# A hybrid decoder layer with x loaded transposed, GpSimd's elementwise work of the first third on VectorE and ScalarE, and conv blocks that leave PSUM by one copy

## The chip, the cores and the metric

The kernel runs on one core of a Trainium2 chip. The metric is device time in microseconds. Three runs of the kernel before took 1224.8, 1224.88 and 1230.06 us; the median is 1224.88. The engines have these names in the profile: PE is TensorE (matmuls and transposes; PEld is its loading of weights), DVE is VectorE, ACT is ScalarE, POOL is GpSimd, SP is SyncE, which issues most DMAs.

## The reference

One decoder layer in float32: 1024 tokens, model width 1024.

```python
hn = rms_norm(h, norm_g[i]); proj = hn @ w_in[i]
rg_x, rg_gate, gq, gk, gv, gz, gb, ga, s5_u, s5_gate = split_columns(proj)
xr = causal_dwconv(rg_x, rg_conv_w[i], rg_conv_b[i])             # width 4
y_rg = rg_lru(xr, ...) * silu(rg_gate)                           # 512 channels
y_gdn = gdn_branch(gq, gk, gv, gz, gb, ga, gdn_conv_w[i], ...)   # 8 heads of 128
y_s5 = s5_ssm(s5_u, ...)                                         # 32 groups of 16 channels, 64 states
z5 = gelu(y_s5); y_s5 = z5 * sigmoid(z5 @ s5_w_glu + s5_b_glu) * silu(s5_gate)
h = h + concatenate([y_rg, y_gdn, y_s5]) @ w_out[i]
h = h + sigmoid(rms_norm(h, ple_norm_g[i]) @ ple_w_gate[i]) * (p[i] @ ple_w_proj[i])
return rms_norm(h, final_norm_g)
```

rg_lru has h_t = a_t h_(t-1) + sqrt(1 - a_t^2) (g_t x_t), with sigmoids r and g of block-diagonal products of the conv's output and a = exp(-8 r softplus(-lambda)). gdn_branch passes q, k, v through the same kind of conv and silu, normalizes q and k, and runs the gated delta rule; its decay between positions i and j is exp(gcum_i - gcum_j) for j up to i, 0 above.

## The kernel before, in words

**Precision and tiling.** Every large product is made of three: each float32 operand is split into a rounded part (hi) and its rest (lo), and hi·hi, lo·hi and hi·lo are summed in PSUM. The normalized x lies transposed in SBUF as hhi and hlo: 128 partitions (channels of one k-tile), 8 k-tiles, 1024 tokens. w_in comes in blocks of 128 output columns. A block is projected in two halves of 512 tokens, each 8 k-tiles × 3 products of 128x512, so 48 products a block (`project`, L426); its result has channels on partitions and tokens along the row. The pool `pp` has two PSUM banks for these halves. Each half leaves PSUM by a task called a drain, which runs on ScalarE.

**Weights.** `weight` (L394) loads one block (wraw), casts it to whi on ScalarE (L402) and subtracts on GpSimd for wlo (L404). The next block's task starts when a block's own is taken (`take`). There are two buffers of whi and wlo and one of wraw.

**x.** `norm_x` (L340) loads x in 8 tiles of 128 tokens by 1024 channels. For two tiles at a time ScalarE squares with a sum along the row (L368), VectorE computes the reciprocal root, VectorE (for 6 tiles, L387) or ScalarE and GpSimd (for 2, L383 and L385) multiply by it and by norm_g, and PE transposes the tile in eight 128x128 pieces (L197), from which `transpose_split` (L328) makes hhi on ScalarE (L336) and hlo on VectorE (L338). A half of the projections may begin when its four tiles are split. In the same stretch the projection of p (`ple_proj`, products named `ph`, `pl`) and the tables of S5 (`s5_base`, `s5_tables`) are made; `outer` (L830 to L834) computes the tables from products of 128x1024: one side on VectorE (names s_Q, s_tmp) and the other, `part_g`, on GpSimd (s_G, s_tmg).

**Blocks with a conv.** `project_conv` (L441) serves the RG-LRU's four blocks and the heads' q, k and v. Its drain copies the half into raw on ScalarE (L462, three zero columns ahead), then writes cy = w3·x + bias from PSUM on ScalarE (L465, L467); VectorE adds the three shifted products from raw (L452). cy has a single buffer, so a drain may only run once the previous user of cy is done (`busy`): in the RG-LRU that is its scan (L663).

**RG-LRU, decay, recurrence.** `rg_post` makes the gates and the scan; its steps max (L653), om = 1 - om (L655, GpSimd) and square root (L657) lie between the gate and the scan. `decay` (L583) makes, for each head, the 1024 columns of exp(gcum_i - gcum_j): a row broadcast by DMA, a subtraction and a triangular mask on GpSimd (L588, L591), Exp on ScalarE (L594), out to DRAM. `solve`, `levels` and `chain` then do the delta rule of a head: triangular inverses, and a recurrence with names V, Sm, R, kd, AQ, each step short 128x128 products on PE and short copies and products on VectorE and ScalarE.

**What sets the order.** The work is written as generators (`Task`), each with a lane (pe, v, a, g, d), and `tick` (L247) is called after each projection product: it prices what has been issued on each engine (`price`, `account`) and lets tasks take their next step when their inputs would be there and their engine free; PRIO gives priorities. `pin` fixes the resulting order of each engine. So the order is settled when the kernel is built, from prices, and each engine runs its own list in order. The projection blocks are issued in one fixed sequence: x0 s0 e0 g0 x1 … g3 (16 blocks of the RG-LRU and S5, with x the conv blocks and e, s, g gates and S5 input), then k of heads 0 to 2, then q, v, z of head 0, then the other heads'. A gdn head's recurrence is filled with the projections of later heads.

## Time and profile before

| | us |
|---|---|
| median of three runs | 1224.88 |
| profiled execution | 1232.72 |
| span of its instructions | 1231.0 |
| PE busy | 1126.6 (92%), 6197 matmuls |
| VectorE busy | 844.9 (69%) |
| ScalarE busy | 536.0 (44%) |
| GpSimd busy | 361.0 (29%) |
| mean granted clock of PE | 0.950 |

The profile is one execution, traced by the hardware. Busy is the time in which an engine had an instruction running; the matmuls overlap their weights' loading, and a busy PE may run at half its clock. The span is cut into five stretches below: up to the first wait for baT (start: x is normalized and split), to the last projection before head 0's recurrence, that recurrence, the other heads, and the out projection with the last part.

### The profile page before, as it was taken

To read this page: it belongs to the slowest core of one execution; us is meant where nothing else is said; L and a number is where in the kernel's file an instruction comes from. 1 tells how busy PE (TensorE), PEld (TensorE's weight loads), DVE (VectorE), ACT (ScalarE), POOL (GpSimd) and SP (SyncE) were. 2 spreads that over 40 slices of the span, in tenths; PEclk is the share of its full clock that TensorE was granted. 3 is DMA by queue.
4 is the path that set the end of the run, shared out by engine and by line. 5 is a ranking of instruction groups with operands and counts; after the bars stand their busy time and mean duration, and the time that the engine had idled before them with its cause. 6 is when DMAs were issued, how large, how long until landed. Compare 5 with 4: busy or idle time off the path is not lost. (4 is left out here: it accounts for less than half of the span.)

```text
span 1231.0 us, 17352 instructions
## 1 busy us (share of the span) xinstructions
PE 1126.6 (92%) x6197; PEld 915.5 (74%) x6197; DVE 844.9 (69%) x1986; ACT 536.0 (44%) x1070; POOL 361.0 (29%) x259
## 2 busy tenths in 40 slices
PE   6659979999969998899999999999988999999996
PEld 5437768778757777788888788888866878878885
DVE  7797697759688894697579857974655344263764
ACT  6514545452646543235443534354564233243432
POOL 4321523416133452011112111221165033044442
PEclk9778989999979998589999999999989999999999
DMA  7301326153465431112222221212255455364222
GB/s 286 120 26 53 97 57 189 54 155 103 135 194 172 148 109 46 31 63 58 76 63 69 69 73 48 86 31 74 102 197 176 166 190 184 122 207 144 89 88 84
DMA packets 81621, 136.49 MB, mean 111 GB/s; under 512 B 31104, under 2 KB 41536, under 8 KB 81536
## 3 DMA queue, kind: packets, MB, share of 16 engines
q1 hardware_dynamic: 80384, 131.20, 34.0%
q0 software_dynamic: 1152, 4.19, 0.9%
q8 instruction: 49, 0.80, 0.3%
q14 instruction: 36, 0.29, 0.1%
HBM read 98.50 MB, written 31.49 MB: 106 GB/s over the span
## 5 line engine op out<-in xcount | busy, mean ns | idle before, releaser
L194 PE MATMUL pp<-hhi,whi 128*128 128x512 f32 x768 | 318.0, 414 | 20.1 <-ACT cy L465 11.1
L194 PE MATMUL pp<-hhi,wlo 128*128 128x512 f32 x768 | 315.6, 411 | 2.1 <-POOL wlo L404 2.1
L194 PE MATMUL pp<-hlo,whi 128*128 128x512 f32 x768 | 316.5, 412 | 0.0
L404 POOL TENSOR_TENSOR wlo<-wraw,whi 128x1024 fp32r<-128x1024 f32 (+1 forms) x52 | 126.7, 2436 | 509.2 <-ACT whi L402 470.2
L194 PEld LDWEIGHTS pp<-hhi,whi 128*128 128x128 f32 x768 | 148.5, 193 | 51.4 <-ACT cy L465 12.4
L194 PEld LDWEIGHTS pp<-hhi,wlo 128*128 128x128 f32 x768 | 147.8, 193 | 31.5 <-issue 2.5
L194 PEld LDWEIGHTS pp<-hlo,whi 128*128 128x128 f32 x768 | 148.1, 193 | 30.0 <-issue 2.9
L452 DVE SCALAR_TENSOR_TENSOR cy<-raw,c_gdn_conv_w,cy 128x512 f32<-128x512 f32 x144 | 130.5, 907 | 13.8 <-ACT cy L465 13.3
L1454 DVE TENSOR_TENSOR mhl<-mr,mhl 128x512 fp32r<-128x512 f32 x64 | 59.2, 925 | 81.9 <-ACT mhl L1452 80.2
L1454 POOL TENSOR_TENSOR ws<-wsr,ws 128x512 fp32r<-128x512 f32 x48 | 67.4, 1407 | 141.0 <-ACT ws L1452 140.9
L194 PE MATMUL pg<-ws,mhl 128*128 128x512 f32 x384 | 101.1, 397 | 0.6 <-ACT mhl L1452 0.4
L194 PEld LDWEIGHTS pg<-ws,mhl 128*128 128x128 f32 x384 | 71.5, 188 | 19.6 <-DVE mhl L1454 1.4
L194 PE MATMUL pp<-ws,fth 128*128 128x512 f32 x256 | 80.6, 395 | 0.0
L1452 ACT CAST mhl<-mr 128x512 fp32r<-128x512 f32 x64 | 39.8, 621 | 86.3 <-DMA mr<-mix 49.9
L402 ACT CAST whi<-wraw 128x1024 fp32r<-128x1024 f32 (+1 forms) x52 | 52.7, 1014 | 52.0 <-DMA wraw<-in_w_blk 50.0
L462 ACT COPY raw<-pp 128x512 f32<-128x512 f32 x56 | 32.6, 583 | 67.8 <-PE pp L194 67.4
L1101 DVE TENSOR_TENSOR sT<-sW,sA 64x31 f32<-64x31 f32 (+15 forms) x124 | 58.9, 475 | 3.3 <-POOL raw L461 1.4
L194 PEld LDWEIGHTS pp<-ws,fth 128*128 128x128 f32 x256 | 48.1, 188 | 10.9
L1276 ACT ACTIVATE osq<-on 128x128 f32<-128x128 f32 x64 | 19.8, 309 | 76.3 <-DVE on L1273 60.3
L1452 ACT CAST ws<-wsr 128x512 fp32r<-128x512 f32 x48 | 29.7, 621 | 51.3 <-DMA wsr<-in_w_out 26.3
L1250 DVE TENSOR_SCALAR V<-pc,bp 128x128 f32<-128x128 f32 x64 | 22.2, 347 | 43.0 <-PE pc L194 42.5
L194 PE MATMUL pp<-ws,ftl 128*128 128x512 f32 x128 | 51.4, 401 | 0.0
(410 smaller groups left out, 2201.8 us busy)
## 6 DMA issues: line engine op xcount, KB each, us to landing
wraw<-in_w_blk SPq DMA_DIRECT2D x48, 512.0 KB, 3.9
mr<-mix SPq DMA_DIRECT2D x64, 256.0 KB, 3.0
dec<-dec SPq DMA_DIRECT2D x16, 512.0 KB, 4.7
wsr<-in_w_out SPq DMA_DIRECT2D x32, 256.0 KB, 2.9
xt<-in_x SPq DMA_DIRECT2D x8, 512.0 KB, 8.9
ppd<-po POOLq DMA_DIRECT2D x8, 512.0 KB, 3.6
gcb<-grow SPq DMA_DIRECT2D x8, 512.0 KB, 4.5
dec<-gcb SPq DMA_DIRECT2D x8, 512.0 KB, 2.9
```

Of the source, the lines that this page charges most:

```text
L194: self.nc.tensor.matmul(**kw)
L402: nc.scalar.copy(out=hi, in_=raw)
L404: nc.gpsimd.tensor_tensor(out=lo, in0=raw, in1=hi.bitcast(F32), op=ALU.subtract)
L452: nc.vector.scalar_tensor_tensor(out=y[:, sl], in0=raw[:, j + sl.start:j + sl.stop], scalar=wconv[:, j:j + 1], in1=y[:, sl], op0=ALU.mult, ...
L462: nc.scalar.copy(out=raw[:, 3 + 512 * half:3 + 512 * half + 512], in_=ps)
L1101: e.tensor_tensor(out=tv, in0=W[:, :n, j:j + 1].to_broadcast([64, n, m]), in1=A[:, j:j + 1, j + 1:].to_broadcast([64, n, m]), op=ALU.mult)
L1250: v.tensor_scalar(out=V, in0=p2, scalar1=bp[:, t:t + 1], scalar2=None, op0=ALU.mult)
L1276: nc.scalar.activation(out=sq, in_=on[:, t, :], func=AF.Square, accum_out=d["so"][:, t:t + 1])
L1452: nc.scalar.copy(out=hl[:, 0, :], in_=raw)
L1454: e.tensor_tensor(out=hl[:, 1, :], in0=raw, in1=hl[:, 0, :].bitcast(F32), op=ALU.subtract)
```

## The change

x arrives transposed from the host (a second input, xT, is x transposed; x itself is still read later), in 16 pieces of 128 channels by 512 tokens. ScalarE squares a piece; PE sums over channels with four products whose weights are 128x128 pieces of the squares and whose moving operand is one column of ones, so that the sums of 128 tokens lie on 128 partitions; VectorE adds over the k-tiles and takes the reciprocal root; four products with the identity spread it over all partitions and along the row (`rb`); and for each k-tile VectorE multiplies x by norm_g and rb, ScalarE casts to hhi, VectorE subtracts for hlo. `project` now waits for each half and k-tile (`hdone`), and the first block of weights is fetched between the halves of x.

GpSimd's subtractions for wlo, its side of the S5 tables and its half of the PLE split go to VectorE; om goes to ScalarE; max becomes the bias of the square root (`least`, 1e-30); the subtraction in `decay` becomes the bias of Exp, which is issued as eight pieces of 128 columns. In `project_conv` the drain is the copy into raw alone, and cy is made from raw, in SBUF, by the conv's task. Two steps of S5 may take a bank from either of two PSUM pools, silu of k waits for S5's tail, and prices and priorities of the planner are set anew (not shown; VectorE's fixed part is dearer by 0.06 to 0.07 us, GpSimd's by 0.06).

```diff
-    def norm_x(self, hpool, sp, startup):
+    def norm_x(self, hpool, sp, startup, key):
         nc = self.nc
...
         self.hlo = hpool.tile([P, KB, S], F32R, name="hlo")
...
         next(startup)
...
+        H = [slice(0, 512), slice(512, 1024)]
+        xt = [self.slot(tag, [P, S], "xt") for tag in ("dec", "dec", "AT", "AT", "raw", "raw", "qT", "qT")]
+        there = {}
+        for half in range(2):
+            if half:
                 next(startup)
...
+                next(startup)
+                self.fetch(key)
+                self.step(self.wtask[key])
+            for k in range(KB):
+                self.account()
+                nc.sync.dma_start(out=xt[k][:, H[half]], in_=self.i["xT"][k * P:(k + 1) * P, H[half]])
+                there[half, k] = self.account()
+            if not half:
+                g = self.load(sp, "norm_g", [P, KB])
+        sq = [self.slot(tag, [P, 2, 512], "xsq") for tag in ("cy", "kd")]
+        def squares(half, box, sums):
+            box.append(self.ps(self.psg, [P, 4, KB]))
+            for k in range(KB):
+                yield "a", lambda: there[half, k] <= self.now
+                z = sq[k % 2][:, k // 2 % 2]
+                nc.scalar.activation(out=z, in_=xt[k][:, H[half]], func=AF.Square)
+                sums.append(self.spawn(colsum(z, box[0], k), "pe", sums[-1:]))
+        def colsum(z, ss, k):
+            for t in range(4):
+                self.mm(out=ss[:, t, k:k + 1], lhsT=z[:, t * P:(t + 1) * P], rhs=self.ones[:, 0:1], start=True, stop=True)
+            yield
+        def scale(half, box, sums):
+            yield "v", lambda: len(sums) == KB and all(t.done for t in sums)
+            ss = sp.tile([P, 4], F32, name=f"xss{half}")
+            nc.vector.tensor_reduce(out=ss, in_=box[0], axis=mybir.AxisListType.X, op=ALU.add)
+            z = self.rstd_of(sp, ss, 1.0 / D, EPS, 4, f"xr{half}", 1)
             while True:
...
                     break
...
+            yield "pe", self.psg
+            rb = self.ps(self.psg, [P, 512], KB)
+            for t in range(4):
+                self.mm(out=rb[:, t * P:(t + 1) * P], lhsT=r[:, t:t + 1].to_broadcast([P, P]), rhs=self.ident, start=True, stop=True)
+            for k in range(KB):
+                self.spawn(split(half, k, rb), "v")
+        def split(half, k, rb):
+            x, hi, lo = (z[:, H[half]] for z in (xt[k], self.hhi[:, k], self.hlo[:, k]))
+            nc.vector.scalar_tensor_tensor(out=x, in0=x, scalar=g[:, k:k + 1], in1=rb, op0=ALU.mult, op1=ALU.mult)
+            yield "a"
+            nc.scalar.copy(out=hi, in_=x)
+            e, lane = nc.vector, "v"
+            yield lane
+            e.tensor_tensor(out=lo, in0=x, in1=hi.bitcast(F32), op=ALU.subtract)
+            self.hdone.add((half, k))
+            self.hleft[half] -= 1
+        for half in range(2):
+            box, sums = [], []
+            self.spawn(squares(half, box, sums), "a", room=lambda half=half: there[half, 0] <= self.now and self.room(self.psg))
+            self.spawn(scale(half, box, sums), "v", room=lambda sums=sums: len(sums) == KB)
...
         nc.scalar.copy(out=hi, in_=raw)
-        yield "g"
-        nc.gpsimd.tensor_tensor(out=lo, in0=raw, in1=hi.bitcast(F32), op=ALU.subtract)
+        yield "v"
+        nc.vector.tensor_tensor(out=lo, in0=raw, in1=hi.bitcast(F32), op=ALU.subtract)
         self.wts[key] = hi, lo
...
         for half in range(2):
-            self.wait(lambda: not self.hleft[half])
             sl = slice(512 * half, 512 * half + 512)
...
             for k in range(KB):
+                self.wait(lambda: (half, k) in self.hdone)
                 for w, h in ((whi, self.hhi), (whi, self.hlo), (wlo, self.hhi)):
...
-    def project_conv(self, blk, wconv, bias, act=None):
+    def project_conv(self, blk, wconv, bias, act=None, after=()):
         nc = self.nc
...
             sl = slice(512 * half, 512 * half + 512)
+            yield "a", lambda: all(t.done for t in busy)
+            nc.scalar.activation(out=y[:, sl], in_=raw[:, 3 + sl.start:3 + sl.stop], func=AF.Identity, scale=wconv[:, 3:4],
+                                 bias=0.0 if bias is None else bias)
+            yield "v"
             for j in (2, 1, 0):
...
             if act:
-                yield "a"
+                yield "a", lambda: all(t.done for t in after)
                 yield from act(y, raw, sl)
...
             nc.scalar.copy(out=raw[:, 3 + 512 * half:3 + 512 * half + 512], in_=ps)
-            yield
-            if bias is None:
-                nc.scalar.activation(out=y[:, sl], in_=ps, func=AF.Identity, scale=wconv[:, 3:4])
-            else:
-                nc.scalar.activation(out=y[:, sl], in_=ps, func=AF.Identity, scale=wconv[:, 3:4], bias=bias)
-        self.project(blk, evac, lambda: all(t.done for t in busy),
-                     lambda half: out.append(self.spawn(conv(half), "v", self.drains[-1:])))
+        self.project(blk, evac, lambda: not self.hleft[1],
+                     lambda half: out.append(self.spawn(conv(half), "d", self.drains[-1:])))
         self.cybusy = list(out)
...
         nc.sync.dma_start(out=self.grow.rearrange("h (t i) -> (h t) i", t=NT), in_=gr)
-        self.gc = gc
+        self.ngc = keep.tile([P, 64], F32, name="ngc")
+        nc.vector.tensor_scalar(out=self.ngc, in0=gc, scalar1=-1.0, scalar2=None, op0=ALU.mult)
...
         yield "g"
-        nc.gpsimd.tensor_tensor(out=gb, in0=gb, in1=self.gc[:, h * NT:(h + 1) * NT].unsqueeze(2).to_broadcast([P, NT, P]),
-                                op=ALU.subtract)
-        yield
-        nc.gpsimd.affine_select(out=gb, in_=gb, compare_op=ALU.is_ge, fill=-1e4, base=0,
+        nc.gpsimd.affine_select(out=gb, in_=gb, compare_op=ALU.is_ge, fill=-1e30, base=0,
                                 pattern=[[0, NT], [1, P]], channel_multiplier=-1)
         yield "a"
-        nc.scalar.activation(out=gb, in_=gb, func=AF.Exp)
+        for t in range(NT):
+            c = h * NT + t
+            nc.scalar.activation(out=gb[:, t, :], in_=gb[:, t, :], func=AF.Exp, bias=self.ngc[:, c:c + 1])
+            if t == 3:
+                yield
         yield "d"
...
         nc.vector.scalar_tensor_tensor(out=om, in0=r, scalar=1.0, in1=T, op0=ALU.add, op1=ALU.mult)
-        yield "v"
-        nc.vector.tensor_scalar(out=T, in0=T, scalar1=1e-30, scalar2=None, op0=ALU.max)
-        yield "g"
-        nc.gpsimd.tensor_scalar(out=om, in0=om, scalar1=-1.0, scalar2=1.0, op0=ALU.mult, op1=ALU.add)
         yield "a"
-        nc.scalar.activation(out=T, in_=T, func=AF.Sqrt)
+        nc.scalar.activation(out=T, in_=T, func=AF.Sqrt, bias=self.least)
+        yield
+        nc.scalar.activation(out=om, in_=om, func=AF.Identity, scale=-1.0, bias=1.0)
         yield "v"
...
             u = self.slot("AT", [P, 8, 8, 16], "s_tmg")
-            yield from outer(G, u, Ag[:, :, 1:9], cre, Bg[:, :, 1:9], cim, 8, g)
-            yield from outer(G0.unsqueeze(2), u[:, :, 0:1, :], Ag[:, :, 0:1], cre, Bg[:, :, 0:1], cim, 1, g)
+            yield from outer(G, u, Ag[:, :, 1:9], cre, Bg[:, :, 1:9], cim, 8, v)
+            yield from outer(G0.unsqueeze(2), u[:, :, 0:1, :], Ag[:, :, 0:1], cre, Bg[:, :, 0:1], cim, 1, v)
...
         next(q)
-        part = self.spawn(part_g(), "g", room=lambda: i == 0 or i - 1 in self.shifted)
+        part = self.spawn(part_g(), "v", room=lambda: i == 0 or i - 1 in self.shifted)
         yield
...
         for q in range(2):
-            yield "pe", self.psg
-            pt = self.ps(self.psg, [P, 4, P], 2)
+            yield "pe", lambda: self.room(self.psg) or self.room(self.psa)
+            pt = self.ps(self.psg if self.room(self.psg) else self.psa, [P, 4, P], 2)
             for k in range(4):
...
         for q in range(2):
-            yield "pe", lambda: shifted.done and self.room(self.psg)
-            pt = self.ps(self.psg, [P, 4, P])
+            yield "pe", lambda: shifted.done and (self.room(self.psg) or self.room(self.psa))
+            pt = self.ps(self.psg if self.room(self.psg) else self.psa, [P, 4, P])
             for k in range(4):
...
             yield
-        y, raw, cv = self.project_conv(16 + h, self.gcw[:, 8 + h, :], None, act)
+        y, raw, cv = self.project_conv(16 + h, self.gcw[:, 8 + h, :], None, act, self.posts[:3] if h < 2 else self.posts)
         d["k"] = self.spawn(self.k_post(h, cv), "d", after=cv[:1] + [self.decays[h]] + ([self.hd[h - 3]["levels"]] if h >= 3 else []))
...
             nc.scalar.copy(out=hi, in_=r)
-            e, lane = (nc.gpsimd, "g") if half else (nc.vector, "v")
+            e, lane = nc.vector, "v"
             yield lane
...
                 startup = self.ple_proj()
-                self.norm_x(hp, cp, startup)
-                self.fetch(order[0])
+                self.norm_x(hp, cp, startup, order[0])
                 g = self.spawn(self.gates(sb, cp), "d")
...
                 self.gdn_setup(cp)
+                self.posts = tiles
                 for h in range(HEADS):
...
     o["x"] = np.asarray(x)[0]
-    o["norm_g"] = np.asarray(norm_g)[0]
+    o["xT"] = o["x"].T
+    o["norm_g"] = np.asarray(norm_g)[0].reshape(KB, P).T
     w = np.asarray(w_in)[0]
```

**Head 0's recurrence on PE.** The rows are those of PE as the last projections ahead of the recurrence's first level end, before:

```order
L194 MATMUL pp<-hhi,wlo 128x512
L194 MATMUL pp<-hhi,whi 128x512
L194 MATMUL pp<-hlo,whi 128x512
L194 MATMUL pp<-hhi,wlo 128x512
L194 MATMUL pg<-Xs,AT 32x32 x16
L194 MATMUL pg<-M_3810,XT 32x32
L194 MATMUL pg<-XT,M_3810 32x32 x2
L194 MATMUL pg<-M_3810,XT 32x32
```

Here pp are projection products (pp<-hhi,wlo is the third of three), pg<-Xs,AT the first of the levels; 84 rows from there on hold no pp. After:

```order
L194 MATMUL pp<-hlo,whi 128x512
L194 MATMUL pp<-hhi,wlo 128x512
L197 MATMUL pg<-ident,kT 128x128
L194 MATMUL pp<-hhi,whi 128x512
L194 MATMUL pg<-Xs,AT 32x32 x16
L194 MATMUL pp<-hlo,whi 128x512
L194 MATMUL pc<-vn,XT 128x128
L194 MATMUL pp<-hhi,wlo 128x512
L194 MATMUL pg<-kT 128x128 x4
L194 MATMUL pp<-hhi,whi 128x512
L194 MATMUL pc<-V,kd 128x128
L194 MATMUL po<-V,AQ 128x128
```

Level products and the first of the chain (pc<-vn,XT, pc<-V,kd, po<-V,AQ) now stand between projections. The first pg<-Xs,AT is 43 rows further up, after 1147 projections of blocks, and pc<-vn,XT comes after 1169; before, both came after 1248. The last six rows of the chain of head 0 stand without projections in the new order too.

**The last piece of x on VectorE.** Before, from the last subtraction for hlo:

```order
L338 TENSOR_TENSOR hlo<-pg,hhi 128x4x128
L800 TENSOR_TENSOR s_small<-s_s_720 128x32
L801 SCALAR_TENSOR_TENSOR s_s_720<-s_s_720,s_c_719 128x32
L802 TENSOR_TENSOR s_c_719<-s_c_719 128x32
L803 TENSOR_TENSOR s_c_719<-s_c_719,s_small 128x32
L804 TENSOR_TENSOR s_R_721<-s_R_721 128x32
L779 TENSOR_SCALAR s_s_720<-s_s_720 64x32
L697 TENSOR_TENSOR s_tmp<-s_w,s_ki 128x8x16
L698 TENSOR_TENSOR s_tmp<-s_w,s_kr 128x8x16
L699 TENSOR_TENSOR s_w<-s_w,s_kr 128x128
L700 TENSOR_TENSOR s_w<-s_w,s_tmp 128x128
L701 TENSOR_TENSOR s_w<-s_w,s_ki 128x128
```

After, from the last but one:

```order
L402 TENSOR_TENSOR hlo<-xt,hhi 128x512
L847 TENSOR_TENSOR s_G<-s_w,s_Ag 128x1024
L849 TENSOR_TENSOR s_tmp<-s_w,s_Bq 128x1024
L849 TENSOR_TENSOR s_tmg<-s_w,s_Bg 128x1024
L851 TENSOR_TENSOR s_Q<-s_Q,s_tmp 128x1024
L851 TENSOR_TENSOR s_G<-s_G,s_tmg 128x1024
L847 TENSOR_TENSOR s_w<-s_w,s_Ag 128x128
L397 SCALAR_TENSOR_TENSOR xt<-xt,c_norm_g,pg 128x512
L849 TENSOR_TENSOR s_tmg<-s_w,s_Bg 128x8x16
L851 TENSOR_TENSOR s_w<-s_w,s_tmg 128x128
L402 TENSOR_TENSOR hlo<-xt,hhi 128x512
```

The last hlo stands behind the products of both sides of the first S5 table (L847 to L851), which are a later row before.

**The drain of the second conv block on ScalarE.** Before:

```order
L945 COPY s_V<-pg 128x512
L402 CAST whi<-wraw 128x1024 x2
L462 COPY raw<-pp 128x512
L467 ACTIVATE cy<-pp,c_rg_conv_b,c_rg_conv_w 128x512
L462 COPY raw<-pp 128x512
L467 ACTIVATE cy<-pp,c_rg_conv_b,c_rg_conv_w 128x512
L893 COPY s_uP<-pp 128x8x64
```

After:

```order
L674 ACTIVATE cy<-cy 128x1024
L482 COPY raw<-pp 128x512 x2
L418 CAST whi<-wraw 128x1024
L910 COPY s_uP<-pp 128x8x64
L468 ACTIVATE cy<-raw,c_rg_conv_b,c_rg_conv_w 128x512 x2
L910 COPY s_uP<-pp 128x8x64
L418 CAST whi<-wraw 128x1024
```

cy is written from raw and no longer from pp, and both copies out of pp stand ahead of both. whi is the cast of a block's weights, s_uP the drain of the S5 block that comes next; cy<-cy is om.

## Rows read from the trace of the kernel before

**Rows 1.** stretches: from:to length, busy us (instructions) PE PEld DVE ACT POOL, clock, DMA, GB/s

```profile
0.00:94.17 94.17, 56.70 (x241) 41.30 (x241) 76.44 (x213) 39.09 (x71) 33.16 (x32) 0.85 0.40 141
94.17:481.89 387.72, 354.44 (x1709) 286.27 (x1708) 308.58 (x583) 192.64 (x268) 138.48 (x87) 0.95 0.40 118
481.89:527.56 45.67, 38.73 (x322) 32.09 (x322) 24.68 (x100) 14.30 (x44) 2.78 (x4) 0.54 0.15 37
527.56:880.00 352.44, 347.39 (x2455) 292.15 (x2455) 259.80 (x729) 157.55 (x441) 63.84 (x53) 1.00 0.21 64
880.00:1231.00 351.00, 329.36 (x1477) 263.64 (x1475) 175.35 (x364) 132.44 (x247) 122.73 (x84) 0.98 0.46 151
```

**Rows 2.** waits of PE: engine, line <- releaser: us in total, times, longest

```profile
PE pg L197 <- DVE hlo L338: 20.6, 4, 10.4
PE pp L194 <- ACT cy L465: 11.1, 4, 6.8
...
PE pp L194 <- ACT cy L467: 8.9, 1, 8.9
...
PE pc L197 <- DVE baT L500: 5.0, 1, 5.0
PE pp L194 <- POOL wlo L404: 2.1, 1, 2.1
```

**Rows 3.** timeline of PE, projections: start, us, instruction, repeats [idle before <-releaser]

```profile
95.19 0.63 PE L194 MATMUL pp<-hlo,whi 128*128 128x512 f32 x1
95.62 0.63 PE L194 MATMUL pp<-hhi,wlo 128*128 128x512 f32 x1
...
475.74 0.39 PE L194 MATMUL pp<-hlo,whi 128*128 128x512 f32 x1
475.97 0.39 PE L194 MATMUL pp<-hhi,wlo 128*128 128x512 f32 x1
```

**Rows 4.** timeline of PE: transposes of x, and narrow products

```profile
50.43 0.60 PE L197 MATMUL pg<-ident,xt 128*128 128x128 f32 x4
50.78 0.48 PE L194 MATMUL pc<-pl,ph 128*128 128x512 f32 x1
...
109.99 0.33 PE L194 MATMUL pc<-gg,upper 128*128 128x64 f32 x2
110.15 0.39 PE L194 MATMUL pc<-gg,ones 128*128 128x64 f32 x2
```

**Rows 5.** timeline of DVE in the first stretch

```profile
26.41 2.40 DVE L725 TENSOR_TENSOR s_small<-s_small 128x32 f32<-128x32 f32 x1
28.85 0.19 DVE L726 SCALAR_TENSOR_TENSOR s_small<-s_small 128x32 f32<-128x32 f32 x1
...
67.61 0.74 DVE L452 SCALAR_TENSOR_TENSOR cy<-raw,c_rg_conv_w,cy 128x512 f32<-128x512 f32 x1
...
81.34 0.68 DVE L338 TENSOR_TENSOR hlo<-pg,hhi 128x512 fp32r<-128x512 f32 x1
...
91.75 1.21 DVE L832 TENSOR_TENSOR s_tmp<-s_w,s_Bq 128x1024 f32<-128x1024 f32 x1
```

**Rows 6.** timeline of ACT: the drain of a conv block that PE waits for

```profile
159.93 0.78 ACT L467 ACTIVATE cy<-pp,c_rg_conv_b,c_rg_conv_w 128x512 f32<-128x512 f32 x1 [4.32 <-DVE rr L663]
```

**Rows 7.** timeline of PE: the projection that follows that drain

```profile
160.77 0.79 PE L194 MATMUL pp<-hhi,whi 128*128 128x512 f32 x1 [8.94 <-ACT cy L467]
```

**Rows 8.** lines of POOL, 0 to 480 us: form, count | busy, mean ns | idle before, releaser

```profile
L404 POOL TENSOR_TENSOR wlo<-wraw,whi 128x1024 fp32r<-128x1024 f32 x27 | 67.5, 2502 | 177.3 <-ACT whi L402 166.3 <-PE pc L197 6.7 <-PE pg L194 4.2
```

**Rows 9.** timeline of POOL beside the first row of Rows 5

```profile
25.55 3.21 POOL L385 TENSOR_TENSOR xt<-xt,gb 128x1024 f32<-128x1024 f32 x1 [2.39 <-ACT xt L383]
```

**Rows 10.** lines of DVE, 0 to 480 us: conv products

```profile
L452 DVE SCALAR_TENSOR_TENSOR cy<-raw,c_gdn_conv_w,cy 128x512 f32<-128x512 f32 x48 | 47.8, 998 | 6.7 <-ACT cy L465 6.5
```

**Rows 11.** timeline of PE: the same product in two steps of head 0's recurrence

```profile
511.70 0.77 PE L194 MATMUL pc<-V,kd 128*128 128x128 f32 x2 [0.53 <-DVE V L1250]
...
515.47 0.77 PE L194 MATMUL pc<-V,kd 128*128 128x128 f32 x2 [0.54 <-DVE sT L1101]
```

More of the change, by code (lines that the diff above doesn't have):

```diff
@@ L55 @@
     AHEAD = (0, 0.3, 0.3, 0)
-    PRIO = dict(turn=2, drain=-1, save=-0.5, conv=1, gates=2, blocks=2, part_g=1, s5_out=1, shift=-1, k_post=1, q_post=1, v_post=-0.5, chain=1, chain_out=-1, finish=1, solve=1, levels=1, glu_prep=0.5, pre=1, glu_post=2, split_late=1, split_soon=-0.5, add=-0.5, ple_norm=2, s5_base=0.5, s5_tables=2, decay=2, decay_late=-1, wstream=-1, mstream=0.5)
+    PRIO = dict(squares=2, colsum=2, scale=2, split=2, drain=-1, save=-0.5, conv=1, gates=2, blocks=2, part_g=1, s5_out=1, shift=-1, k_post=1, q_post=1, v_post=-0.5, chain=1, chain_out=-1, finish=1, solve=1, levels=1, glu_prep=0.5, pre=1, glu_post=2, split_late=1, split_soon=-0.5, add=-0.5, ple_norm=2, s5_base=0.5, s5_tables=2, decay=2, decay_late=-1, wstream=-1, mstream=0.5)
     def __init__(self, tc, ins, out):
@@ L358, in turn @@
-        def turn(x, t):
-            tl = slice(t * P, (t + 1) * P)
-            yield from self.transpose_split(x, self.hhi[:, :, tl], self.hlo[:, :, tl], self.psg)
-            self.hleft[t // 4] -= 1
-        def rows(t0, n):
-            ss = sp.tile([P, n], F32, name=f"xss{t0}")
-            for t in range(n):
-                yield "a", lambda: there[t0 + t] <= self.now
-                junk = self.slot("cy", [P, D], "xsq")
-                nc.scalar.activation(out=junk, in_=xt[t0 + t], func=AF.Square, accum_out=ss[:, t:t + 1])
-            yield "v"
-            z = self.rstd_of(sp, ss, 1.0 / D, EPS, n, f"xr{t0}", 1)
+        H = [slice(0, 512), slice(512, 1024)]
```

38 lines of the change are left out of this document (7 added, 31 removed).

## The prediction

> **What bounds the kernel now.** I read the table of stretches first [rows 1]: busy time of each engine in five stretches, then TensorE's clock. TensorE (PE) is busy in nearly all of it, so the time is PE work plus PE idle, and the change can only gain from idle time or from clock. Idle time lies in three places: 0 to 94.17 us (56.70 busy, 37.5 idle), 94.17 to 481.89 (354.44 of 387.72, 33.3 idle), and after 880 (329.36 of 351.00), which the change hardly touches. From 527.56 to 880 PE is busy 347.39 of 352.44; nothing is to be had there. The fourth place is a matter of clock: 481.89 to 527.56 is 38.73 us of PE work at a granted clock of 0.54, near the lower of its two levels (1.2 of 2.4 GHz), so 38.73 × 0.54 = 20.9 us at full clock. That stretch holds no projection, only the recurrence of head 0: many short products, each waiting for VectorE.
>
> Then the list of what PE waited for [rows 2]. 20.6 us go to the split x (hlo, four waits). 11.1 + 8.9 = 20.0 us go to cy, written by ScalarE from PSUM: a drain that stands behind a recurrence of VectorE. 5.0 us go to baT. Only 2.1 us in the whole run go to wlo of GpSimd.
>
> The two prices of a projection are in [rows 3]: it repeats every 0.227 us at full clock (475.74 to 475.97), every 0.425 at the half clock (95.19 to 95.62).
>
> **Stage 1, x.** *Removed:* 64 transposes of 128x128. Four take 50.78 − 50.43 = 0.35 us [rows 4], so 16 × 0.35 = 5.6 us of PE; also the wait of a whole half for its last piece, since half 1 may begin when its first k-tile is split. *Added on PE:* 64 column sums, 128x1 with 128 columns of weights, and 8 broadcasts of 128x128. The trace has no 128x1 matmul; the nearest is a 128x64 with the same weights, two in 0.16 us there counted as one fp32 product (109.99 to 110.15) [rows 4]. Bounds: 0, if they fall in the 37.5 idle us, and 0.43 each at the half clock's price of a 512-column step [rows 3], 27.5 us. I take 64 × 0.16 = 10.2 us, the row that it is nearest to, and 8 × 0.09 for the broadcasts (the transposes' price). Net +5.3 us of PE work, nearly all of it ahead of 82 us, where PE idles.
>
> The Trainium skill, "TensorE: Matmul & The Clock Gate", section "Step-by-step: what each phase is for", says that the time to load weights follows their column count. By it a 128x1 product with 128 columns of weights is not the hundredth part of a wide one; if it did follow the moving columns, the 64 would cost under 1 us and the sum be some 5 us lower where they aren't hidden. The 0.16 us row has both loads in it and can't tell the two apart.
>
> *What the end of the stage does.* The last hlo ended at 82.0 us before (81.34 + 0.68) [rows 5]. In the new order of VectorE it stands behind five table products of 1.21 us [rows 5] (6 us) that came after it or were GpSimd's, while the squares leave ScalarE in 512-column pieces and two chains of rsqrt replace four. I take 82 to 86 us. By then 21 of the 24 products of half 1 are out, where none was: 21 × 0.227 = 4.8 us. baT is now needed after 66 projections and not 43, so 5.0 us go; the fourteen steps at half clock behind that wait (95.19 on) cost 14 × 0.2 = 2.8 us, which go too. 12.6 us saved, less about 6 for a later last hlo and the sums: **−6 us**, from −20 (no later hlo, all added PE work hidden, more of the 20.6 saved) to +15 (sums at 0.43, hlo at 90).
>
> **Stage 2, 94 to 482 us.** *Conv leaves by one copy.* The activation that wrote cy from PSUM had to wait till cy's last reader, the scan on VectorE, was done; in the rows the drain starts at 159.93, 4.32 us after ScalarE was free, ended by the scan [rows 6], and PE resumes at 160.77 after 8.94 us [rows 7]. With the copy into raw alone, PSUM waits for nothing that VectorE does. So 20.0 us of waits go, and with each the slow clock that followed (the stretch has 0.95). What is late next: VectorE, which is 308.58 of 387.72 us busy [rows 1], and whose longest chain is still scan, then conv.
>
> *wlo and the tables on VectorE.* Of the 27 wlo up to 480 us [rows 8] about 24 lie here: 24 × 1.21 = 29 us (price of a 128x1024 product of two SBUF operands, 91.75 [rows 5]). part_g four times: three of 1.21 and three an eighth as wide (0.3, a guess from their size), 4 × 4.5 = 18 us. The max goes, four times 1.21 at most, 4 us taken. Added to VectorE +43 us. Against it stands what GpSimd took from VectorE. At 26.41 a 128x32 product on VectorE lasted 2.40 us, the next one 0.19, while GpSimd's own product ran 25.55 to 28.76 [rows 5, 9]. And 48 conv products take a mean of 1.00 us [rows 10], where one of that shape took 0.74 (67.61) [rows 5]: 48 × 0.26 = 12 us. The 24 of the RG-LRU and the other forms with two SBUF operands (scans, tables, S5) I put at twice that, 25 us, an estimate by the same share. So VectorE stays about as full as it was (+43 − 37), and wlo itself takes 1.21 us where it took 2.50.
>
> The Trainium skill warns here: "Perfetto Trace Analysis", section "Optimizing Scalar/DVE Operations", says that VectorE and GpSimd share an SBUF read port, so that moving work between the two might not help, and that a full VectorE should rather hand work away. The trace agrees that they hold each other up (2.40 against 0.19 us); whether work comes back as time is the rival below.
>
> The other edits I cost at nothing, because the projections on PE cover them: decay's subtract goes from GpSimd into the bias of Exp, now eight pieces, and om goes to ScalarE, which is busy for only 192.64 of 387.72 us [rows 1]; were ScalarE late by it, the conv's copies would be, some 1 us for each of eight heads. The four subtracts of PLE on VectorE lie in the start's 37.5 idle us.
>
> Waits added: wlo now stands in VectorE's queue behind convs and scans. PE has one block's 48 × 0.227 = 10.9 us to spare, since the weights of the next block are fetched as this one starts. The sum: 20.0 gone, some 6 of clock gone, 8 come back as new waits for VectorE: **−18 us**, from −35 (all 33.3 idle us and clock) to +10 (the wlo late by 0.6 us in each of 47 blocks, 28, against the 18).
>
> **Stage 3, head 0's recurrence.** In the order before, the first of its products comes after all 1248 projections of its first part, and 84 rows of PE follow with none; now the levels come after 1147 and the chain's first product after 1169, woven between the rest. So 101 projections, 23 us, now lie beside a recurrence whose steps wait on VectorE: before, one step of the chain took 515.47 − 511.70 = 3.8 us, with a wait of half a us in each [rows 11]. At best the stretch shrinks to its 20.9 us of work, −24.8. The last few steps are still bare; I leave 8 to 9 us of that exposed: **−16 us**, from −25 to 0 (if PE, in order, waits at each step for VectorE).
>
> **The rest** is as before: 0, give or take 5.
>
> **Sum.** −6 − 18 − 16 = −40. The profiled execution took 1232.72 us (span 1231.0), so 1192.7. The median of three is 1224.88, 0.6% less: 1192.7 × 1224.88 / 1232.72 = **1185 us**.
>
> **Rivals.**
> *VectorE becomes the bound.* The +43 us count in full where the conv chains run, the lost contention doesn't come back there, and head 0 isn't ready earlier than PE reaches it: stage 3 gives 0, stage 2 −8, stage 1 −6. −14: 1218.7, on the median's scale 1211. For it: VectorE 308.58 busy of 387.72 already. Against: the 1.00 against 0.74 us of a conv product [rows 10, 5]. The page of the Trainium skill named above would have it so.
> *wlo late at every block (slower).* The place is PE's third product of a block, which needs wlo; VectorE is in order, and a scan, such as ended the 4.32 us of [rows 6], or a train of tables may stand ahead; behind wlo on that queue stand the convs that the next drains feed. The gain of 40 us is spent over 47 blocks at 40 / 47 = 0.85 us each, from there it is slower; at 1.2 us it is −40 + 56 = +16: 1248.7, 1241. For it: ScalarE's and VectorE's in-order queues made the 8.94 us wait [rows 7]. Against: a block's 10.9 us of lead, and only 2.1 us of such waits before [rows 2].
> *No change.* The column sums come at the half clock and the last hlo late, +15; stage 2 −8, stage 3 −7: 0, 1225.
>
> **Numbers.** Forecast 0.62 (own range 1165 to 1205), VectorE 0.20, slower 0.11, no change 0.07. All three terms at their low ends would give 1145, at their high ends 1250; three ends at once are unlikely. The range reaches to 1226 to take in the VectorE case and no change and down to 1160; left out are the slower case and small tails. About 0.5% (6.1 us) is what three runs from 1224.8 to 1230.06 can tell. Faster 0.80 (0.02 of the VectorE case falls under the bound), same 0.09, slower 0.11.
>
> **What would show it.** Right: no wait of PE for cy; the last hlo at 82 to 86 us; conv products near 0.8 us; a granted clock near 1 after 482 us, with projections up to within 10 us of the end of head 0's chain. Wrong: waits of PE for wlo or for x in hundreds of ns per block, column sums of 0.4 us, a bare stretch of recurrence at half clock as long as before, or VectorE over 90% busy before 480 us.

## The result, and the profile after

The changed kernel took 1245.76 us in the median of four runs (1243.39 to 1249.87), the kernel before 1226.78 in its four; the ratio is 1.0156 [1.0117, 1.0194]. Forecast was 1185, so the sign was wrong.

Stretches, cut at the same places of the work in both kernels: the first product of block 1, of block 19 (q of head 0), of block 26 (after head 0's recurrence) and of block 47 (the last). The third stretch so holds some 96 us, of the kernel before, that the prediction counted to its second stage. Columns as in [rows 1]; before:

```profile
0.00:97.32 97.32, 59.85 (x248) 43.78 (x249) 78.15 (x218) 39.09 (x71) 33.16 (x32) 0.84 0.39 137
97.32:385.93 288.61, 260.26 (x1279) 209.36 (x1277) 226.01 (x392) 143.86 (x180) 97.28 (x60) 0.95 0.41 119
385.93:527.56 141.63, 129.76 (x749) 106.52 (x747) 105.54 (x285) 63.08 (x132) 43.98 (x31) 0.83 0.30 94
527.56:881.63 354.07, 349.02 (x2465) 293.50 (x2464) 260.74 (x731) 157.55 (x441) 63.84 (x53) 1.00 0.21 64
881.63:1231.00 349.37, 327.73 (x1468) 262.30 (x1466) 174.41 (x362) 132.44 (x247) 122.73 (x84) 0.98 0.46 152
```

After:

```profile
0.00:105.92 105.92, 79.54 (x320) 62.83 (x321) 64.74 (x211) 39.94 (x71) 9.18 (x20) 0.85 0.36 121
105.92:400.73 294.81, 259.88 (x1310) 209.94 (x1309) 216.57 (x479) 157.86 (x227) 12.82 (x19) 0.95 0.43 124
400.73:525.82 125.09, 109.96 (x725) 89.76 (x723) 83.23 (x243) 63.68 (x141) 9.46 (x17) 0.95 0.30 88
525.82:879.88 354.06, 348.12 (x2453) 294.10 (x2453) 253.29 (x751) 157.50 (x438) 12.66 (x30) 1.00 0.21 66
879.88:1244.60 364.72, 337.13 (x1478) 270.22 (x1476) 180.68 (x371) 133.39 (x250) 114.62 (x80) 0.96 0.42 144
```

By these, +8.6 us at the start (forecast −6), +6.2 in the middle (−18), −16.5 round head 0's recurrence (−16, its clock back at 0.95), 0.0 in the heads, and +15.3 at the end (0), where of the edited code only four subtractions for wlo and half a conv block stand.

The waits of PE after, as in [rows 2]:

```profile
PE pg L194 <- DVE s_X L989: 13.6, 1, 13.6
PE pg L194 <- ACT xsq L369: 10.9, 1, 10.9
PE pg L194 <- DVE AT L1093: 9.2, 1, 9.2
PE pp L194 <- ACT hhi L399: 8.3, 5, 2.2
...
PE pp L194 <- DVE hlo L402: 3.9, 4, 1.6
```

No wait for cy is left, and none for wlo. s_X, which is the last S5 tile's state, now has the longest wait.

PE meets that wait in a hole between projections. In both kernels the code has, behind the k blocks (block 18 is their last), `self.need(*tiles, *outs)`: block 19 is laid out only when all steps of S5 have been laid out. Before, from the last product of block 18 to the first of block 19:

```profile
382.65 0.39 PE L194 MATMUL pp<-hhi,wlo 128*128 128x512 f32 x1
385.01 1.16 PE L194 MATMUL pg<-kT 128*128 128x128 f32 x8 [1.97 <-DVE AT L1076]
385.93 0.48 PE L194 MATMUL pp<-hhi,whi 128*128 128x512 f32 x1
```

After, with the row of the stretch between:

```profile
357.84 0.39 PE L194 MATMUL pp<-hhi,wlo 128*128 128x512 f32 x1
...
391.38 0.77 PE L194 MATMUL pg<-s_X,s_G 128*128 128x128 f32 x2 [13.62 <-DVE s_X L989]
...
400.73 0.48 PE L194 MATMUL pp<-hhi,whi 128*128 128x512 f32 x1
```

```profile
357.84:400.73 42.89, 13.34 (x82) 12.36 (x81) 22.32 (x72) 14.71 (x34) 5.92 (x5) 0.68 0.46 117
```

At the end of block 18 PE was 25 us ahead of the kernel before; at block 19 it was 15 us behind. The hole has 13.34 us of PE's work in 42.89 us.

VectorE's conv and scan, against [rows 10] and, for the scan, this row of the kernel before:

```profile
L663 DVE TENSOR_TENSOR_SCAN rr<-cy,rT 128x1024 f32<-128x1024 f32 x4 | 13.3, 3324 | 0.2
```

After:

```profile
L472 DVE SCALAR_TENSOR_TENSOR cy<-raw,c_gdn_conv_w,cy 128x512 f32<-128x512 f32 x39 | 29.2, 753 | 9.1 <-ACT cy L468 5.8 <-issue 3.1
...
L680 DVE TENSOR_TENSOR_SCAN rr<-cy,rT 128x1024 f32<-128x1024 f32 x4 | 9.1, 2285 | 0.9 <-ACT cy L674 0.8
```

A conv product fell from 998 to 753 ns and a scan from 3324 to 2285: VectorE's own pace came back, as forecast.

The start, on PE: column sums at its early pace, and later (four sums are eight instructions):

```profile
13.60 1.70 PE L194 MATMUL pg<-ones,xsq 128*128 128x1 f32 x8
15.16 0.78 PE L194 MATMUL pp<-ph,pl 128*128 128x512 f32 x1
...
50.99 0.95 PE L194 MATMUL pg<-ones,xsq 128*128 128x1 f32 x8
51.80 0.48 PE L194 MATMUL pg<-ph,pl 128*128 128x512 f32 x1
```

That is 0.39 and 0.20 us a sum. And the last pieces of x on VectorE, which [rows 5] had done at 82.0:

```profile
95.73 0.69 DVE L402 TENSOR_TENSOR hlo<-xt,hhi 128x512 fp32r<-128x512 f32 x1
96.34 1.22 DVE L847 TENSOR_TENSOR s_G<-s_w,s_Ag 128x1024 f32<-128x1024 f32 x1
...
100.88 1.22 DVE L851 TENSOR_TENSOR s_G<-s_G,s_tmg 128x1024 f32<-128x1024 f32 x1
...
103.64 0.69 DVE L402 TENSOR_TENSOR hlo<-xt,hhi 128x512 fp32r<-128x512 f32 x1 [0.16 <-ACT hhi L399]
```

### The profile page after: what moved, and what is told of

It reads as the page before. It is cut to its first block, busy times and chain, and to the rows that moved or that the text cites. A ratio compares the mean times of both kernels' runs of the same rounds, so it can differ in the third digit from the quotient of the medians.

```text
span 1244.6 us, 17541 instructions
## 1 busy us (share of the span) xinstructions
PE 1134.6 (91%) x6277; PEld 926.8 (74%) x6277; DVE 798.5 (64%) x2051; ACT 552.4 (44%) x1127; POOL 158.7 (13%) x166
## 5 line engine op out<-in xcount | busy, mean ns | idle before, releaser
L472 DVE SCALAR_TENSOR_TENSOR cy<-raw,c_gdn_conv_w,cy 128x512 f32<-128x512 f32 x144 | 107.3, 746 | 11.3 <-ACT cy L468 7.3
L1471 DVE TENSOR_TENSOR mhl<-mr,mhl 128x512 fp32r<-128x512 f32 x64 | 53.2, 833 | 93.1 <-ACT mhl L1469 93.1
L420 DVE TENSOR_TENSOR wlo<-wraw,whi 128x1024 fp32r<-128x1024 f32 (+1 forms) x52 | 63.1, 1213 | 46.6 <-ACT whi L418 44.1
L194 PE MATMUL pp<-ws,mhl 128*128 128x512 f32 x192 | 52.5, 408 | 3.2 <-ACT mhl L1469 2.1
L1293 ACT ACTIVATE osq<-on 128x128 f32<-128x128 f32 x64 | 19.6, 307 | 64.9 <-DVE on L1290 50.0
```

The source lines that it names most:

```text
L194: self.nc.tensor.matmul(**kw)
L420: nc.vector.tensor_tensor(out=lo, in0=raw, in1=hi.bitcast(F32), op=ALU.subtract)
L472: nc.vector.scalar_tensor_tensor(out=y[:, sl], in0=raw[:, j + sl.start:j + sl.stop], scalar=wconv[:, j:j + 1], in1=y[:, sl], op0=ALU.mult, ...
L1293: nc.scalar.activation(out=sq, in_=on[:, t, :], func=AF.Square, accum_out=d["so"][:, t:t + 1])
L1471: e.tensor_tensor(out=hl[:, 1, :], in0=raw, in1=hl[:, 0, :].bitcast(F32), op=ALU.subtract)
```

## The experiments

Times are medians; ratios are to the kernel before, measured on the same chip. Differences in us are between medians, some of them from different chips; the median of the kernel before lay between 1226.8 and 1228.7 there, so 2 us between two runs say nothing. "x as before" is rows, transposes and the old split; "the old prices" are those of the planner before. X·G is the product of an S5 tile's state s_X with its table s_G.

**Undoing one part of the changed kernel.**

`u_x`: the diff of `norm_x`, `hleft` and `project` taken back, as

```diff
...
+            self.wait(lambda: not self.hleft[half])
...
-                self.wait(lambda: (half, k) in self.hdone)
...
```

> The changed kernel with x loaded in rows again, transposed and split as before; all else as changed. Theory 1 (the S5 chain is the bound of the first 400 us, and the new start, with its 64 column sums and with x's pieces in turn with the S5 tables on VectorE, sets it back): the first X·G product of S5 comes about 10 us earlier (185 to 175), the last gelu of S5 likewise, and the kernel takes 8 to 12 us less than the changed one, 1234 to 1238. Rival (VectorE's work in the first stretch is what counts, not x): within 4 us of the changed kernel.

1221.36, 0.9932 [0.9908, 0.9956]: 24 us. Block 1 started at 78.7 us, not 105.9; but S5's first X·G product only 6 us sooner (179.2), its last gelu 26 us (384.6). The start is confirmed, its size twice what I expected.

`u_price`:

```diff
-            return 0.16 + n / (460 if op == "InstTensorTensor" else 860)
+            return 0.1 + n / (445 if op == "InstTensorTensor" else 860)
...
-        return (0.19 if op == "InstTensorScalarPtr" and n > 64 else 0.14) + n / 960
+        return (0.13 if op == "InstTensorScalarPtr" and n > 64 else 0.07) + n / 960
```

> The changed kernel with the planner's old prices. Theory 2 (the 15 us lost after 880 us, where no instruction was changed, come from another order of the last head's products and of the streams behind them, which the planner's new prices set): the stretch from the last block's first product to the end goes back from 365 towards 349 us, the rest stays, and the time is 1230 to 1236. Rival (that order follows from where the earlier work left off, whatever the prices): the tail stays within 5 us of 365.

1211.53, 0.9856 [0.9828, 0.9884]: 34 us, with the same instructions (17541 in both profiles). Its stretches, cut at the same places:

```profile
0.00:105.74 105.74, 87.03 (x313) 69.65 (x314) 60.43 (x205) 38.05 (x69) 9.18 (x20) 0.94 0.35 121
105.74:389.05 283.31, 259.06 (x1317) 209.25 (x1316) 222.03 (x488) 156.58 (x221) 9.56 (x18) 0.96 0.44 125
389.05:508.20 119.15, 108.94 (x725) 89.34 (x724) 89.41 (x250) 64.41 (x149) 11.89 (x20) 0.94 0.33 101
508.20:857.50 349.30, 346.58 (x2461) 291.90 (x2460) 255.52 (x744) 161.92 (x441) 12.46 (x28) 1.00 0.22 66
857.50:1209.50 352.00, 330.39 (x1468) 264.69 (x1466) 177.61 (x366) 131.82 (x247) 117.02 (x80) 0.97 0.45 149
```

The end (block 47 on) took 352.0 us and not 364.7, but that is 13 of the 34; of the rest 11.5 lie in the middle, 5.9 round head 0 and 4.8 in the heads, and none at the start. From the first product of block 47 to the first of the out projection it took 60.9 us and not 69.64. Lines of VectorE in that stretch (form, count | busy, mean ns | idle before, releaser), of the changed kernel and then of this one:

```profile
L1308 DVE TENSOR_TENSOR on<-on,ory 128x512 f32<-128x512 f32 x3 | 5.5, 1841 | 0.0
...
L1267 DVE TENSOR_SCALAR V<-pc,bp 128x128 f32<-128x128 f32 x10 | 3.5, 349 | 10.7 <-PE pc L194 10.7
```

```profile
L1267 DVE TENSOR_SCALAR V<-pc,bp 128x128 f32<-128x128 f32 x8 | 2.8, 346 | 9.6 <-PE pc L194 9.6
...
L1308 DVE TENSOR_TENSOR on<-on,ory 128x512 f32<-128x512 f32 x2 | 2.5, 1235 | 0.0
```

With the dear price ten steps of the recurrence (V) and three finishing products (on) were left when the last block began, with the old one eight and two: the recurrences stand later between the projections, and their last steps are bare for longer.

`u_partg`:

```diff
-            yield from outer(G, u, Ag[:, :, 1:9], cre, Bg[:, :, 1:9], cim, 8, v)
+            yield from outer(G, u, Ag[:, :, 1:9], cre, Bg[:, :, 1:9], cim, 8, nc.gpsimd)
...
-        part = self.spawn(part_g(), "v",
+        part = self.spawn(part_g(), "g",
```

> The changed kernel with GpSimd's side of the four S5 tables back on GpSimd; all else as changed. Theory 1 (VectorE serves both x's pieces and the S5 tables, and both are late by it): the last hlo comes 5 to 10 us sooner than 104 us, S5's last gelu before 405 us instead of 410, and the time falls by 5 to 10 us, to 1236 to 1241. Rival (GpSimd's port costs VectorE what the tables cost): within 3 us.

1241.84, 1.011 [1.0083, 1.0138]: 4 us, and the last hlo later (112.1): the theory's mechanism isn't seen; inconclusive.

`u_decay`, the diff of `decay` taken back, of which this is the Exp:

```diff
...
-        for t in range(NT):
-            nc.scalar.activation(out=gb[:, t, :], in_=gb[:, t, :], func=AF.Exp, bias=self.ngc[:, c:c + 1])
...
+        nc.scalar.activation(out=gb, in_=gb, func=AF.Exp)
```

> The changed kernel with decay as before: the subtraction on GpSimd and one Exp of 1024 columns, not eight pieces with a bias. Theory 3 (S5's last tile is late by 19 us since ScalarE, in order, waits 5.6 us for a decay's row and mask at 331 us with S5's copies behind it, and SP's queue waits for Exp likewise): the last tile's period, from X·G of the third to X·G of the fourth, falls from 71.5 us towards 53, and the time by 8 to 15 us, to 1231 to 1238. Rival (the waits move with the planner's order and aren't of decay's making): that period stays above 65 us and the time within 5 us.

1234.9, 1.0045 [1.0023, 1.0067]: 11 us, but the period was 64.9 us: between the two, and `uxp_udecay` below speaks for the rival.

**Both large ones, and the rest on that base.** `ux_uprice` is `u_x` with the old prices.

> The changed kernel with both x as before and the planner's old prices. Theory 1+2 (the start cost 25 us and the prices 34, at different places): the two add up, 1246 - 25 - 34 = 1187, between 1182 and 1195. Rival (both free the same S5 chain, so the second finds little left): 1200 to 1211.

1181.28, 0.9638 [0.9604, 0.9673]: they add up, and 65 us separate it from the changed kernel. Its stretches to block 47:

```profile
0.00:83.90 83.90, 56.59 (x248) 41.20 (x249) 66.13 (x223) 39.77 (x71) 14.86 (x21) 0.90 0.46 159
83.90:360.58 276.68, 256.67 (x1303) 208.35 (x1301) 220.48 (x483) 154.72 (x220) 10.97 (x19) 0.97 0.46 130
360.58:473.90 113.32, 107.38 (x723) 88.08 (x723) 89.03 (x254) 64.54 (x148) 11.72 (x20) 0.98 0.34 101
473.90:824.87 350.97, 347.81 (x2462) 292.94 (x2462) 253.65 (x740) 161.66 (x441) 11.73 (x28) 1.00 0.22 66
```

Against before: −13.4, −11.9, −28.3, −3.1 us. In the second of them the hole ahead of block 19 is still there: the last product of block 18 began at 333.08 and the first of block 19 at 360.58, 27.5 us apart.

`uxp_uconv`, the diff of `project_conv` taken back (with it goes the wait of k's silu for S5's tail):

```diff
...
+                nc.scalar.activation(out=y[:, sl], in_=ps, func=AF.Identity, scale=wconv[:, 3:4], bias=bias)
-        self.project(blk, evac, lambda: not self.hleft[1],
+        self.project(blk, evac, lambda: all(t.done for t in busy),
...
```

> x as before, the old prices, and the conv blocks leave PSUM as before, by the copy and by the activation that waits for cy; the moves off GpSimd stay. My step said that the one copy frees 20 us of PE's waits for cy and some clock. Theory 5 (it does, and PE's time in the first 390 us hangs on it): 15 to 25 us slower than 1181, waits of PE for cy near 20 us. Rival 5b (S5's chain sets block 19, so PE that is free earlier waits there): within 6 us of 1181.

1201.34, 0.9783 [0.9761, 0.9806]: the one copy is worth 20 us, and waits for cy are back, 14.2 us in place of the 20 that I expected:

```profile
PE pp L194 <- ACT cy L465: 14.2, 2, 9.3
```

`uxp_uwlo_upartg`, with `u_partg`'s edit and

```diff
...
-        nc.vector.tensor_tensor(out=lo, in0=raw, in1=hi.bitcast(F32), op=ALU.subtract)
+        nc.gpsimd.tensor_tensor(out=lo, in0=raw, in1=hi.bitcast(F32), op=ALU.subtract)
```

> x as before, the old prices, and wlo and GpSimd's side of the S5 tables back on GpSimd; the conv by one copy, decay, the RG-LRU's edits stay as changed. Theory 4 (work taken from GpSimd comes back to VectorE as shorter products, so the move is worth its VectorE time): 10 to 20 us slower than the kernel with both undone and the moves kept, conv products at 0.85 us or more in place of 0.75. Rival (the port gives back just what the moves cost): within 4 us of it.

1211.07, 0.9858 [0.982, 0.9897]: the two moves off GpSimd are worth 30 us together. With them VectorE runs 76 instructions more (2063 against 1987) and is busy for less, 805.3 us against 824.8. Conv products took 797 and 843 ns here, scans 2698; of heads and RG-LRU, in this kernel:

```profile
L456 DVE SCALAR_TENSOR_TENSOR cy<-raw,c_gdn_conv_w,cy 128x512 f32<-128x512 f32 x45 | 35.9, 797 | 17.1 <-ACT cy L452 16.7
...
L456 DVE SCALAR_TENSOR_TENSOR cy<-raw,c_rg_conv_w,cy 128x512 f32<-128x512 f32 x24 | 19.8, 843 | 2.8 <-ACT cy L452 2.7
```

The heads' conv products, at 797, stay under the 850 that the theory asked for: most of their fall from 998 is there with wlo and the tables on GpSimd. The larger differences are in 128x1024 products of the RG-LRU and of S5, such as this one, here and then in `ux_uprice`:

```profile
L660 DVE SCALAR_TENSOR_TENSOR rT<-rr,rT 128x1024 f32<-128x1024 f32 x4 | 9.2, 2306 | 2.2 <-ACT rT L656 2.2
```

```profile
L660 DVE SCALAR_TENSOR_TENSOR rT<-rr,rT 128x1024 f32<-128x1024 f32 x4 | 4.9, 1219 | 0.0
```

How much of the 30 us comes by these, how much by wlo being ready sooner, and which of the two moves gave it, isn't shown; with the new prices the tables alone back on GpSimd were 4 us faster, not slower (`u_partg`).

`uxp_udecay`, with `u_decay`'s edit:

> x as before, the old prices, and decay as before (subtraction on GpSimd, one Exp). In the changed kernel that edit cost 11 us. Theory 3 (eight Exp pieces and their table loads on ScalarE are a loss wherever they stand): 1168 to 1176 against 1181. Rival 3b (that loss hung on the dearer prices' order): 1179 to 1190.

1184.94, 0.9655 [0.9624, 0.9685]: no loss here. What decay costs hung on the plan it stood in.

**What of x costs.** `split0_uprice`, with the old prices and

```diff
-    PRIO = dict(squares=2, colsum=2, scale=2, split=2, ...
+    PRIO = dict(squares=2, colsum=2, scale=0, split=0, ...
```

> The changed kernel with the old prices, x transposed as changed, and the planner's priority of scale and split at 0 and not 2, so that VectorE takes x's pieces ahead of the S5 tables. Theory 1a (the new start is late since x's pieces and the S5 tables, at equal priority, take turns on VectorE): the last hlo comes at 75 to 85 us and not at 102, block 1 at 85 to 92 and not 106, the time 1192 to 1203 against 1211. Rival 1b (the start is late from PE's column sums at half clock and the late first projections): block 1 stays after 100, the time 1207 to 1215. Rival 1c (the tables are then late, and S5's chain with them): the last hlo comes early but X·G of the first tile later than 187, and the time is 1207 or more.

1206.99, 0.9831 [0.9792, 0.987]. The last hlo came at 75.2, not 102.2, and bought 4.5 us, within the intervals: theory 1a fell. Block 0 still began at 72.7 and X·G at 184.3.

`cs32r`, with the old prices and

```diff
-        sq = [self.slot(tag, [P, 2, 512], "xsq") for tag in ("cy", "kd")]
+        sq = [self.slot(tag, [P, 2, 512], "xsq", F32R) for tag in ("cy", "kd")]
+        one = sp.tile([P, 2], F32R, name="onr")
...
-                self.mm(out=ss[:, t, k:k + 1], lhsT=z[:, t * P:(t + 1) * P], rhs=self.ones[:, 0:1], start=True, stop=True)
+                self.mm(out=ss[:, t, k, :], lhsT=z[:, t * P:(t + 1) * P], rhs=one, start=True, stop=True)
```

> The changed kernel with the old prices, and the squares and the column of ones rounded to fp32r (two columns of ones, one pass in place of two); the sums are then those of rounded squares. Theory 1b (the column sums' own PE time, 0.39 us each at half clock, holds up the first projections): they take half, block 0 starts some 10 us sooner than 80.5, and the time is 1200 to 1206 against 1211. Rival (S5's tables on VectorE set the start's length, PE has slack): block 0 sooner or not, block 19 within 3 us of 389 and the time within 4 us of 1211.

1195.75, 0.9733 [0.9706, 0.976]: 16 us. Four sums took 0.71 us at the early pace, not 1.56:

```profile
13.50 0.85 PE L194 MATMUL pg<-onr,xsq 128*128 128x2 f32 x4
14.21 0.77 PE L194 MATMUL pp<-ph,pl 128*128 128x512 f32 x1
```

Block 0 began at 53.5, not 80.5. By the spacing of the rows on PE ahead of block 0, the sums took 8.3 us in all and not 25.1, and the 112 products of 512 columns that both kernels have there took 32.5 us and not 40.8. So PE's own time for the sums was two thirds of the 27 us, and its pace nearly all of the rest: with the float32 sums among them, products stood 0.43 us apart till 68 us in `u_price`,

```profile
66.94 0.63 PE L194 MATMUL pp<-pl,ph 128*128 128x512 f32 x1
67.37 0.63 PE L194 MATMUL pp<-ph,pl 128*128 128x512 f32 x1
...
68.11 0.40 PE L194 MATMUL pp<-pl,ph 128*128 128x512 f32 x1
68.34 0.40 PE L194 MATMUL pp<-ph,pl 128*128 128x512 f32 x1
```

and in `cs32r` they first came to 0.23 at 24.5 us, with 22 of the 112 at the slow spacing and not 57. Why the pace rose later there isn't shown.

`price1`, with the old prices and, in `price`,

```diff
+            if n == 1:
+                return 0.2
```

> The changed kernel with the old prices, but the planner prices a product with one moving column at 0.2 us and not at 0.01. Theory 1d (the planner laid out the first 50 us as if 64 column sums took no time, so that PLE's products and copies stand in the way of block 0): block 0 starts 8 us or more before 80.5, and the time is 1200 to 1206. Rival (PE's time is spent whatever the plan): block 0 at 77 or later, and the time 1207 to 1214.

1205.56, 0.9818 [0.9787, 0.9848]: block 0 came at 68.5, and the time is 6 us less than with the old prices alone, though the intervals touch. A plan that knows the sums' price is perhaps part of it.

`x_best`: `cs32r` with `scale=0, split=0` and a price of 0.1 for the two-column product.

> x transposed, old prices, rounded squares and ones (the sums of rounded squares), their products priced at 0.1 us, and scale and split at priority 0. If the start's loss is the column sums and the plan that took them for free, this equals x as before, 1178 to 1186; if transposed x has another cost (two roots' chains in series with 16 casts and subtractions), it stays at 1190 to 1197.

1175.69, 0.9573 [0.9548, 0.9597], the fastest of all, with the squares in the norm rounded: with cheap sums transposed x costs nothing against x as before (0.9638), and perhaps gains a little.

**What of the prices costs.** `u_pdve`: VectorE's old price alone.

> The changed kernel with VectorE's old price alone, GpSimd's new. Theory 2a (VectorE's dearer fixed part makes the planner put products later behind VectorE than need be, and spread VectorE's steps): nearly all of the price's 34 us come back, 1209 to 1218. Rival 2b (GpSimd's price, or any small change, shuffles the order): 1225 or more.

1212.73, 0.9878 [0.9856, 0.9901]: it is VectorE's.

`p_late` is `ux_uprice` with

```diff
+        if self.count > 2256:
+            return (0.19 if op == "InstTensorScalarPtr" and n > 64 else 0.14) + n / 960
```

and `p_early` has `<=` there; 2256 projection products are those of the blocks 0 to 46.

> x as before, and the dearer VectorE price only from the last projection block on (the last head's recurrence, the out projection, PLE). Theory 2 (the tail's loss is those prices at work there): 12 to 18 us above 1181, with 47 us and more from block 47 to the first out product in place of 60, all of the loss behind block 47. Rival (the tail's order follows from where the heads before left it): within 4 us of 1181.

1181.98, 0.9626 [0.9601, 0.9651]: theory 2 as I had it fell; alone, the dear price at the end costs nothing that can be told.

> x as before, and the dearer VectorE price only up to the last projection block, the old one behind it. Theory 2: 40 us were lost with the dearer price throughout (1221 against 1181), so 22 to 28 us are lost here, all ahead of block 47, spread over S5's chain and the heads. Rival (the dear price matters at the tail alone): within 4 us of 1181.

1197.9, 0.9759 [0.9723, 0.9795]: 17 us, all ahead of block 47, fewer than expected. `ux_ppool` is `u_x` with GpSimd's old price:

> x as before, VectorE's dearer price throughout, GpSimd's old price. The dearer VectorE price cost 17 us up to block 47 (1198), 1 us behind it (1182), and both new prices 40 us throughout (1221). If the 23 us that are missing come from the early and the late stretch together (the last heads start from a worse order): 1215 to 1224. If they are GpSimd's price: 1195 to 1203.

1204.07, 0.9819 [0.9792, 0.9847], nearer to the second: throughout, VectorE's price costs 23 us, and GpSimd's another 17, though only about 1 with x transposed. The costs don't add up: each price gives another plan as a whole.

## Why the prediction was wrong

The waits for cy went, VectorE's own pace came back and head 0's recurrence lies between projections, as I had it. But the agreement in size is in good part luck. My terms for the middle and head 0 were −18 and −16, −34 together; `ux_uprice` measured −11.9 and −28.3, −40.2, and no run has the new order of head 0 by itself. The moves off GpSimd, which I had at +43 and −37 us of VectorE's time and at no gain, were worth 30 us, more than the one copy with its 20. The time forecast, 1185, is that of the kernel without x's new start and without the new prices: 1181.

Three steps failed.

*Stage 1, "I take 64 × 0.16 = 10.2 us, the row that it is nearest to".* Eight groups at 1.56 us, and the eight of half 1 from 39.45 on, 7.9 us, are 20.4 us; the eight broadcasts took 2.4, not 0.7. So PE got 17 us more work and not 5.3 (20.4 + 2.4 - 5.6), towards the upper bound that I had put down (27.5) and then left: 0.16 was a price at the full pace, where a sum took 0.20, and more than half of the sums ran at the slow one, at 0.39. The second half of the step, "nearly all of it ahead of 82 us, where PE idles", failed too: the sums stand in PE's order between PLE's products and ahead of block 0, which came 14 us later, and on the old prices 25. Idle time hides work only where that work is not in front of what the stage waits for. The last hlo, at 104.3 and not 82 to 86, was wrong by more but cost little (`split0_uprice`).

*Stage 2, "So 20.0 us of waits go", and "What is late next: VectorE, ... whose longest chain is still scan, then conv".* The waits went, but what came next was the end of S5's chain, behind which the code holds block 19. PE came there 25 us ahead and stood in the hole of 42.89 us, so the stretch grew by 6.2 us where I had −18. With the old prices and x as before the hole is 27.5 us, and the stretch −11.9. That the barrier makes the hole is read from the code and from PE's order; no run moved it.

*"The rest is as before: 0, give or take 5"*, and with it the edits that I had named "not shown": the planner's prices. I read the order for three places, and took it that the planner would do as well with other prices. VectorE's fixed part, 0.06 to 0.07 us dearer per instruction, cost 34 us (`u_price`, `u_pdve`). The likely way, which no run shows by itself: in the plan each step behind VectorE comes later, and on queues that run in order other work stands ahead of it. It shows in every stretch but the start, and most in the last, beside code that was hardly touched.

None of the rivals was right. "wlo late at every block" gave 1241, nearest to the 1245.76 measured, by chance: no such wait exists after. "VectorE becomes the bound" (1211) fits neither the time nor VectorE, which up to block 19 was busy for 281 of 401 us, against 304 of 386 before. It was right that chains through VectorE come next, and S5's is one: its last gelu began at 410.5 us against 385.0. The plan and the start lengthened it, not the added work on VectorE, for with that work it came at 361.8 in `ux_uprice`.

By the Trainium skill, "Perfetto Trace Analysis", section "Optimizing Scalar/DVE Operations", work moved between VectorE and GpSimd might not help; here it gave 30 us (`uxp_uwlo_upartg`).

What stays open: what ends S5's chain sooner, or lets PE do later blocks meanwhile (27 us in the best of these kernels, too); how the dear price makes 17 us early, 1 late and 23 throughout, and why GpSimd's price costs 17 us with one start and 1 with the other. Only the plans as wholes were measured.

## What to carry to other kernels

A planner's prices are part of the change: price them back first, since that takes one run and was worth 34 us here, more than either edit that was measured by itself. Price a product with few moving columns from a row with the same weights, not by its columns, and at the pace that PE has at that place. Ask of every wait that goes what PE will stand at next: look for places where the code holds back all later work, and for the chain that ends last there. Where work leaves GpSimd for VectorE, compare VectorE's mean times beside GpSimd's work and away from it before calling the move a loss.
